# Hybrid decoder block: the denominators of forgetting attention by GpSimd, the first filler's weights loaded sooner, the last norm by halves

## The chip, the cores and the metric

The kernel runs on one core of one Trainium2 chip. A core has five engines with a queue of instructions each: TensorE (PE, matrix products, with a second queue PEld for weight loads), VectorE (DVE), ScalarE (ACT), GpSimd (POOL) and SyncE (SP, used here to issue transfers). Operands live in SBUF, products are summed in eight PSUM banks of 128 partitions by 512 float32, and the large tensors are in HBM. Engines wait for each other by semaphores. The metric is the device time of one execution in microseconds (us); smaller is better.

## What is computed

One decoder layer on 1024 tokens of width 1024, all in float32: two attentions side by side on the same normed input, merged by gates, then a SwiGLU feed-forward part and a final norm.

```python
h = rms_norm(x, norm_mix_g)
proj = h @ w_in                                   # q, k, v of both attentions, forget logits, gates
# dilated attention: 3 groups (window, dilation) x 4 heads of 64, softmax with ALiBi bias,
# the groups mixed by the softmax of their log-sum-exp -> o_a
# forgetting attention: 8 heads of 64, causal
c = cumsum(log_sigmoid(f_logit))                  # per head, along the sequence
logit[t, s] = q[t] . k[s] / sqrt(64) + c[t] - c[s]    for s <= t
o_b = softmax(logit) @ v
merged = sigmoid(..) * (o_a @ w_dil_out) + sigmoid(..) * (o_b @ w_fox_out)
x = x + merged @ w_out
gu = rms_norm(x, norm_ffn_g) @ w_ffn_in           # 2 x 2816 columns
x = x + (silu(gu[:, :2816]) * gu[:, 2816:]) @ w_ffn_down
out = rms_norm(x, norm_final_g)
```

## The kernel before

Float32 precision comes from splitting: an operand is written as a rounded part (`hi`, by ACT, L99) and a remainder (`lo`, by DVE, L102), and a product becomes three products with 128x512 moving operands: hi by hi, hi by lo, lo by hi (L110 to L112, or L315 in the block products `prod`). Large projections are computed from 2x2 blocks with seven block products instead of eight (`projections`, L315). So almost all the time is a row of 128x512 products on PE.

The program runs in stages: value projections and the norm (to about 130 us), the other projections (to about 311 us), forgetting attention (to about 511 us), dilated attention (from 485 us, overlapping, to 621 us), merge and output projection, the feed-forward part, and from 1424 us the rest of the final norm.

**Forgetting attention** has eight units: four head pairs `pr` times two halves `b` of the queries. For a unit, `fox_scores` (L700 on) computes for each head of the pair the scores of 512 queries against 4 or 8 blocks of 128 keys, keys on the partitions: two products each (L713, L714) into a bank, a copy with bias by ACT (L717) into the tile `L`, a causal mask by POOL on diagonal blocks (L720), and a running maximum over key blocks by DVE (L727) into one quarter of the tile `mx`. Then POOL takes the maximum over the 128 partitions (L728, a `partition_all_reduce`, whose result stands in every partition). `fox_values` belongs to the unit before: `fox_exp` subtracts the maximum (DVE, L741 and L744), takes the exponential (ACT, L747), and sums the exponentials over key blocks into the same quarter of `mx` (DVE, L751 and L753). Then come the products with the values (L765) into the bank `po`, and two products of a 128x64 tile of ones with the two heads' sums (L769) into the bank `den`: they add the sums over the 128 partitions and put each head's denominator on its 64 partitions of the bank. `finish` (L371 on) turns `den` into a reciprocal, by Ln and Exp on ACT (L378, L379, tile `rc`) and one Newton step on DVE (L381, L382), and scales `po` with it (L384); POOL issues the store.

Between these products stand **fillers** (`ahead`, L240): projections that attention itself does not need yet (gate columns, and two of the dilated attention's keys, the list `BESIDE`), 48 products each, into banks `pf`. They give PE work while a softmax is under way. The order of each engine's queue is set when the program is built, by a list scheduler that simulates the engines with its own costs, and by explicit constraints (`issue_after`: not before a given instruction; the list `beside` holds the steps of the fillers, to be interleaved). The first filler's weights are loaded by SP (L123), split by ACT and DVE (L99, L102) and used from 290.94 us on, among the last block products and the first scores.

**Dilated attention** follows the same pattern: a maximum over partitions by POOL (L860), sums by DVE (L876), values (L916) and its own products of ones (L922), which the change leaves alone.

**The final norm** works row block by row block of 128 tokens as the last products come out. For each half of 512 columns, DVE adds the bank to the residual (L1359) and ACT squares it with a sum over the row (L1429), which writes the squares into `xf` as well. After the second half, DVE adds the two sums (L1433) and multiplies the whole row of 1024 by the gain into `xf` (L1434); `rstd` takes the square root on ACT (L150) and the rest on DVE (L147, L151 to L160); then ACT and DVE scale a half each (L1439, L1441), and two transfers store them (L1443).

Of the kernel before, what the change touches and what calls it, by code (L numbers as in the profile page):

```python
# [8 lines left out]
F32 = mybir.dt.float32  # L9
F32R = mybir.dt.float32r  # L10
# [37 lines left out]
def layer_kernel(  # L48
# [60 lines left out]
    def mm3(psum, w, m, start, stop):  # L109
        nc.tensor.matmul(psum, w.hi, m.hi, start=start, stop=False)  # L110
        nc.tensor.matmul(psum, w.hi, m.lo, start=False, stop=False)  # L111
        last_mm[0] = nc.tensor.matmul(psum, w.lo, m.hi, start=False, stop=stop)  # L112
# [6 lines left out]
    def load_w(src, kt, n, tag="w", pool=None, rpool=None):  # L119

        hi, lo = [(pool or wpool).tile([P, kt, -(-n // P) * P], F32R, tag=tag + h, name=nm("w" + h), bufs=2) for h in "hl"]
        raw = (rpool or wpool).tile([P, kt, n], F32, tag="wr", name=nm("wr"), bufs=2)
        last_w[0] = nc.sync.dma_start(out=raw[:], in_=src.rearrange("(k p) c -> p k c", p=P))  # L123
        split(hi[:], lo[:], raw[:])
        return Pair(hi, lo)
# [114 lines left out]
    def ahead(pool, c0, dst, dl=1, sc=1.0):  # L240

        pf = [psf.tile([P, HALF], F32, tag="f", name=nm("pf")) for _ in range(2)]
        w = load_w(w_in[:, c0:c0 + P], KT, P)
        steps = []
        for hh in range(2):
            for k in range(KT):
                mm3(pf[hh][:], w[:, k], hT[hh][:, k], k == 0, k == KT - 1)
                steps.append(last_mm[0].ins)
        beside.append(steps)
        n = HALF // dl  # L250
        for hh in range(2):
            st = pool.tile([P, dl, n], F32, tag="fst", name=nm("fst"), bufs=2)
            stored.append(nc.scalar.activation(out=st[:], in_=view(pf[hh][:], dl), func=AF.Copy, scale=sc).ins)
            nc.scalar.dma_start(out=residues(dst, dl, hh), in_=st[:])
# [32 lines left out]
    def left_side(pool, rg, ru, bufs, a22_bufs=2, first=False):  # L287
# [20 lines left out]
        with tc.issue_after(s12_hi[0].ins) if first else ExitStack():  # L308
            return A1, S12, fill(S34, s34[:]), fill(A22, u2)

    def prod(bank, a, b, first=False):
        for k in range(4):
            w, m = a[:, k], b[:, k]
            for n, (p, q) in enumerate(((w.hi, m.hi), (w.hi, m.lo), (w.lo, m.hi))):
                last_mm[0] = nc.tensor.matmul(bank[:], p, q, start=first and k == 0 and n == 0,  # L315
                                              stop=k == 3 and n == 2, skip_group_check=True)

    def projections(pool, T, c, dst, dls, sc, hl=False, first=False):

        T1, T2, T3, T4 = T  # L320

        def put(i, hh, op):

            st = pool.tile([P, dls[i], HALF // dls[i]], F32, tag="qo", name=nm("qo"), bufs=4)
            op(st[:], dls[i])
            if hl:
                flat = st[:].rearrange("p r i -> p (r i)")
                hi = pool.tile([P, HALF], F32R, tag="qh", name=nm("qh"), bufs=2)
                split(hi[:], flat, flat)
                d = dst[i][:, :, hh * HALF:(hh + 1) * HALF]  # L330
                nc.scalar.dma_start(out=d[0], in_=hi[:].bitcast(F32))
                nc.gpsimd.dma_start(out=d[1], in_=flat)
            else:
                nc.gpsimd.dma_start(out=residues(dst[i], dls[i], hh), in_=st[:])

        cc, v2, v3 = [pool.tile([P, HALF], F32, tag=n, name=nm(n), bufs=1) for n in ("cc", "v2", "v3")]
        A1, S12, S34, A22 = left_side(pool, *[raw_w(w_in[:, c0:c0 + P]) for c0 in c], 1, 2, first)
        b1, b2, b3 = pd(), pd(), pd()

        def copy(out, bank, r=1):  # L340
            nc.scalar.activation(out=out, in_=view(bank[:], r), func=AF.Copy, scale=sc)  # L341

        def join(out, bank, other, r=1):
            p, q = view(bank[:], r), view(other[:], r)
            if sc == 1.0:
                nc.vector.tensor_tensor(out=out, in0=p, in1=q, op=ALU.add)
            else:
                nc.vector.scalar_tensor_tensor(out=out, in0=p, scalar=sc, in1=q, op0=ALU.mult, op1=ALU.add)

        flat = view(cc[:], 1), view(v2[:], 1), view(v3[:], 1)  # L350
        prod(b1, A1[:, :4], B11, True)
        with tc.issue_after(s12_hi[0].ins) if first else ExitStack():
            copy(flat[0], b1)
        prod(b2, S12[:, 4:], T2, True)
        join(flat[1], b2, cc)
        prod(b1, A1[:, 4:], B21)
        put(0, 0, lambda o, r: copy(o, b1, r))
        prod(b2, S34[:, :4], T3)
        join(flat[2], b2, cc)
        prod(b3, S12[:, :4], T1, True)  # L360
        put(1, 1, lambda o, r: join(o, b3, v3, r))
        prod(b2, A22, T4)
        put(1, 0, lambda o, r: join(o, b2, cc, r))
        prod(b3, S34[:, 4:], B22)
        put(0, 1, lambda o, r: join(o, b3, v2, r))
# [251 lines left out]
    w0_ctx.__exit__(None, None, None)  # L617

    with pool_of("proj", 1) as upool:
        reserve(upool, ("qh", [HALF], F32R, 2), *[("a22" + n, [4, P], F32R, 2) for n in "hl"],  # L620
                *[(t, [HALF], F32, 1) for t in ("cc", "v2", "v3")], ("qo", [HALF], F32, 4),
                *[("s34" + n, [KT, P], F32R, 1) for n in "hl"], ("pad", [HALF], F32, 1))
        for pr in range(0, 4, 2):
            for a in range(2):
                c0 = FOX0 + a * FOX_W + pr * P
                projections(upool, T, (c0, c0 + P), [fqk_dram[a, pr + i] for i in range(2)], (1, 1),
                            (SCALE, 1.0)[a], True, pr + a == 0)
        for two in TWOS:
            projections(upool, T, [dil_cols(*t) for t in two], [dqk_dram[t] for t in two],
                        [STR[a][g] for u, g, a in two], (SCALE, 1.0)[two[0][2]])  # L630

# [16 lines left out]
    with pool_of("attention", 1) as apool:  # L650
# [104 lines left out]
        def fox_values(pool, scs, pr, b):  # L755

            nj = 4 * b + 4
            for sc in scs:
                fox_exp(sc, b)
            po, den = pd(), pd()  # L760
            fox_valued.append([])
            for j in range(nj - 1, -1, -1):
                for e in (1, 0):
                    L, _, width, off = scs[e]
                    fox_valued[-1].append(nc.tensor.matmul(  # L765
                        po[half[e], HALF - width[j]:], vf[j // 4][:, j % 4, pr, e], L[:, off[j]:off[j + 1]],
                        start=(j == nj - 1), stop=(j == 0), skip_group_check=True).ins)
            for e in (1, 0):
                nc.tensor.matmul(den[half[e], :], ones[:, :64], scs[e][1], start=True, stop=True)  # L769
            o = pool.tile([P, HALF], F32, tag="o", name=nm("o"), bufs=2)  # L770
            finish(pool, po, den, o[:])
            nc.gpsimd.dma_start(out=o_dram[2 + pr, :, b * HALF:(b + 1) * HALF], in_=o[:])
# [524 lines left out]
    with pool_of("down", 1) as fpool, pool_of("early", 1, side="right") as epool:  # L1297
# [121 lines left out]
        with tc.issue_after(last_xr[0].ins):  # L1419
            nc.gpsimd.dma_start(out=gainf[:], in_=norm_final_g.unsqueeze(0).broadcast_to([P, D]))  # L1420
        parts = {}

        def last_rows(t, ch, out, pt):
            add(out, pt)
            if ch == 0:
                parts["xf"] = fpool.tile([P, D], F32, tag="xf", name=nm("xf"), bufs=3)
            xf = parts["xf"]
            sq = parts[ch] = small.tile([P, 1], F32, tag="sq", name=nm("sq"))
            nc.scalar.activation(out=xf[:, ch * HALF:(ch + 1) * HALF], in_=out, func=AF.Square, accum_out=sq[:])  # L1429
            if ch == 0:  # L1430
                return
            ss = small.tile([P, 1], F32, tag="ss", name=nm("ss"))
            nc.vector.tensor_tensor(out=ss[:], in0=parts[0][:], in1=parts[1][:], op=ALU.add)  # L1433
            nc.vector.tensor_tensor(out=xf[:], in0=acc[t][:], in1=gainf[:], op=ALU.mult)  # L1434
            r = rstd(ss, True)
            for c in range(2):
                cs = slice(c * HALF, (c + 1) * HALF)
                if c == 0:
                    nc.scalar.activation(out=xf[:, cs], in_=xf[:, cs], func=AF.Copy, scale=r[:, 0:1])  # L1439
                else:  # L1440
                    nc.vector.tensor_scalar(out=xf[:, cs], in0=xf[:, cs], scalar1=r[:, 0:1],  # L1441
                                            scalar2=None, op0=ALU.mult)
                (nc.scalar, nc.sync)[c].dma_start(out=out_rows(t)[:, cs], in_=xf[:, cs])  # L1443
# [34 lines left out]
```

## Time and profile before

| | us |
|---|---|
| median of 3 runs (lowest, highest) | 1437.19 (1435.22, 1440.91) |
| the profiled execution | 1435.33 |
| its span in the trace | 1432.6 |
| time around the span (difference) | 2.7 |

| stage, us from the span's start | PE busy | DVE busy | ACT busy | POOL busy |
|---|---|---|---|---|
| 280 to 310, last projections | 30.00 of 30 | 12.51 | 4.76 | 12.38 |
| 620 to 1424, merge to last product | 803.77 of 804 | 488.70 | 296.77 | 297.08 |

The table's rows come from one question about busy time in windows; a PE that is busy in all of a window means that products followed each other there without a gap. The windows of the attention stages are shown with the prediction. A 128x512 product is shown as 389 ns long, but they are pipelined: in a row of them one starts every 0.227 us.

### The profile page before, as it was taken

The numbers are of one execution on the slowest core, as the hardware profiler recorded it, in microseconds if no ns is written. First come the engines' busy times: TensorE is split into PE (matmuls) and PEld (weight loads), VectorE is DVE, ScalarE is ACT, GpSimd is POOL, SyncE is SP. The second block draws the span as 40 slices with busy tenths as digits, with TensorE's granted clock in tenths as the row PEclk, the third lists the DMA queues.
The fourth block names the chain that finished last, engine by engine and source line by source line (L and its number), as shares of the span: only waits on it lengthen the run. The fifth ranks groups of instructions, "written<-read, shape, count | busy, mean of one in ns | idle before, by whom it ended". The sixth has DMA issues, their size and how long they took to land.

```text
span 1432.6 us, 18278 instructions
## 1 busy us (share of the span) xinstructions
PE 1421.4 (99%) x6826; PEld 1154.6 (81%) x6826; DVE 946.9 (66%) x1331; ACT 564.0 (39%) x841; POOL 486.6 (34%) x435
## 2 busy tenths in 40 slices
PE   9999999999999999999999999999999999999997
PEld 7888888887776777778888888888888888888886
DVE  6484654459989899967547755565555665765755
ACT  5333433236666523454235522223232233534333
POOL 1021444435434212100454145666666664000000
PEclk9999999999999999999999999999999999999999
DMA  7232444475534462345796223223332332966512
GB/s 243 67 111 75 153 162 125 129 223 133 140 112 118 147 235 67 120 160 176 288 355 253 74 81 103 95 91 101 101 105 97 110 125 96 390 220 226 203 40 80
DMA packets 162407, 212.51 MB, mean 148 GB/s; under 512 B 13712, under 2 KB 110992, under 8 KB 162064
## 3 DMA queue, kind: packets, MB, share of 16 engines
q1 hardware_dynamic: 126304, 119.06, 26.1%
q0 software_dynamic: 15040, 54.54, 10.5%
q10 hardware_dynamic: 20976, 37.76, 8.3%
q8 instruction: 53, 0.87, 0.2%
q14 instruction: 34, 0.28, 0.1%
HBM read 145.79 MB, written 65.54 MB: 148 GB/s over the span
## 4 chain that ended last, share of the span: by engine, by line
PE 95%; DVE 3%; DMA 1%; ACT 0%; issue 0%; POOL 0%; SPq 0%; DVEq 0%; POOLq 0%
PE pd L315 31%; PE pd L1393 11%; PE pf L315 8%; PE pd L110 6%; PE pd L111 6%; PE pd L112 6%; PE pf L110 4%; PE pf L112 4%; PE pf L111 4%; PE pd L203 2%; PE pd L207 2%; PE pd L204 2%; PE pd L765 2%; PE pd L713 1%; PE pd L916 1%; PE pd L714 1%
## 5 line engine op out<-in xcount | busy, mean ns | idle before, releaser
L315 PE MATMUL pd<-tT,wh 128*128 128x512 f32 x768 | 234.8, 389 | 0.0
L102 DVE TENSOR_TENSOR wl<-wr,wh 128x1024 fp32r<-128x1024 f32 (+2 forms) x106 | 125.0, 1181 | 112.2 <-ACT wh L99 112.0
L99 ACT ACTIVATE wh<-wr 128x1024 fp32r<-128x1024 f32 (+2 forms) x106 | 91.1, 861 | 261.3 <-PE pd L315 170.0
L315 PEld LDWEIGHTS pd<-tT,wh 128*128 128x128 f32 x768 | 144.1, 188 | 29.9
L315 PE MATMUL pd<-hT_t,wh 128*128 128x512 f32 x536 | 165.5, 389 | 0.0
L315 PE MATMUL pd<-tT,wl 128*128 128x512 f32 x384 | 147.6, 389 | 0.0
L315 PEld LDWEIGHTS pd<-hT_t,wh 128*128 128x128 f32 x536 | 100.4, 188 | 21.2 <-ACT cc L341 0.2
L110 PE MATMUL pf<-hT_t,wh 128*128 128x512 f32 x288 | 114.3, 397 | 0.0
L111 PE MATMUL pf<-hT_t,wh 128*128 128x512 f32 x288 | 112.5, 391 | 0.0
L112 PE MATMUL pf<-hT_t,wl 128*128 128x512 f32 x288 | 112.3, 390 | 0.0
L99 ACT ACTIVATE wh<-s 128x1024 fp32r<-128x1024 f32 x58 | 61.4, 1060 | 110.0 <-POOL s L302 82.0
L315 PE MATMUL pd<-hT_t,wl 128*128 128x512 f32 x268 | 104.3, 389 | 0.0
L99 ACT ACTIVATE oh<-raw 128x1024 fp32r<-128x1024 f32 x66 | 70.0, 1062 | 81.0 <-PE pd L1393 34.2
L301 POOL TENSOR_TENSOR s<-wr 128x512 f32<-128x512 f32 x29 | 53.3, 1837 | 139.5 <-DMA wr<-in_w_in_dram 67.8
L315 PE MATMUL pf<-hT_t,wh 128*128 128x512 f32 x320 | 98.7, 389 | 0.0
L102 DVE TENSOR_TENSOR wl<-s,wh 128x1024 fp32r<-128x1024 f32 x58 | 71.8, 1239 | 27.7 <-ACT wh L99 27.7
L1393 PE MATMUL pd<-ol,oh 128*128 128x512 f32 x224 | 87.1, 389 | 0.0
L1393 PE MATMUL pd<-oh,ol 128*128 128x512 f32 x224 | 86.3, 389 | 0.0
L1393 PE MATMUL pd<-oh 128*128 128x512 f32 x224 | 84.7, 389 | 0.0
L315 PEld LDWEIGHTS pd<-tT,wl 128*128 128x128 f32 x384 | 72.1, 188 | 15.0
L1085 POOL TENSOR_TENSOR r<-r 128x512 f32<-128x512 f32 x32 | 43.7, 1379 | 116.2 <-DVE wl L102 95.9
L102 DVE TENSOR_TENSOR ol<-raw,oh 128x1024 fp32r<-128x1024 f32 x66 | 76.5, 1221 | 6.6 <-ACT oh L99 6.3
(331 smaller groups left out, 3228.8 us busy)
## 6 DMA issues: line engine op xcount, KB each, us to landing
wr<-in_w_in_dram SPq DMA_DIRECT2D x46, 512.0 KB, 4.6
wr<-in_w_ffn_in_dram SPq DMA_DIRECT2D x44, 512.0 KB, 3.8
raw<-left_dram SPq DMA_DIRECT2D x56, 256.0 KB, 5.3
g_dram<-fst ACTq DMA_DIRECT2D x32, 256.0 KB, 2.2
r<-in_w_ffn_down_dram SPq DMA_DIRECT2D x8, 1024.0 KB, 8.9
right_dram<-r POOLq DMA_DIRECT2D x8, 1024.0 KB, 7.4
left_dram<-f POOLq DMA_DIRECT2D x8, 1024.0 KB, 4.7
raw<-right_dram SPq DMA_DIRECT2D x32, 256.0 KB, 5.4
```

The source lines that it names most:

```text
L99: last_hi[0] = nc.scalar.activation(out=hi, in_=src, func=AF.Copy)
L102: last_lo[0] = nc.vector.tensor_tensor(out=lo, in0=src, in1=hi.bitcast(F32), op=ALU.subtract)
L110: nc.tensor.matmul(psum, w.hi, m.hi, start=start, stop=False)
L111: nc.tensor.matmul(psum, w.hi, m.lo, start=False, stop=False)
L112: last_mm[0] = nc.tensor.matmul(psum, w.lo, m.hi, start=False, stop=stop)
L203: nc.tensor.matmul(pt[hh][:], w.hi[:, k], m.hi, start=(k == 0), stop=False)
L204: nc.tensor.matmul(pt[hh][:], w.hi[:, k], m.lo, start=False, stop=False)
L207: nc.tensor.matmul(pt[hh][:], w.lo[:, k], m.hi, start=False, stop=(k == kt - 1))
L301: nc.gpsimd.tensor_tensor(out=s12[:, :4], in0=u1, in1=u2, op=ALU.add)
L315: last_mm[0] = nc.tensor.matmul(bank[:], p, q, start=first and k == 0 and n == 0, stop=k == 3 and n == 2, skip_group_check=True)
L1085: nc.gpsimd.tensor_tensor(out=out, in0=p, in1=q, op=ALU.subtract)
L1393: nc.tensor.matmul(bank[:], p, q, start=new and n == 0 and i == 0, stop=n == last and i == 2, skip_group_check=True)
```

## The change

Three edits.

1. In `fox_values`, the products of ones are gone. For each head, POOL sums the head's quarter of `mx` over the partitions with an add `partition_all_reduce` in place (new L776). The two heads' results stand in full in two quarters; ACT copies the second head's on partitions 64 to 127 into the first quarter (new L778, a copy of 64x512), and `finish` reads that quarter instead of a PSUM bank. A unit takes one PSUM bank instead of two.
2. The weights of the first filler are loaded ahead, right after the load of the weights of the last but one pair of projections (`TWOS[-2]`), into the space of the `qh` tiles, and are split there; `ahead` takes them from `w_beside`. `qh` becomes one tile with two halves that are used in turn. The products of the first filler are placed not before a given block product (the 49th from the end, `block_steps[-49]`), and `prod` records its products for that.
3. In the last norm, ACT's squares go to a tile of their own (`squares`, from the ring of three `xf` buffers), and DVE multiplies each half by the gain right after its add, instead of the full row after both.

```diff
     def ahead(pool, c0, dst, dl=1, sc=1.0):
-        w = load_w(w_in[:, c0:c0 + P], KT, P)
+        w = w_beside.pop() if w_beside else load_w(w_in[:, c0:c0 + P], KT, P)
...
             for k in range(KT):
-                mm3(pf[hh][:], w[:, k], hT[hh][:, k], k == 0, k == KT - 1)
+                with ExitStack() if beside else tc.issue_after(block_steps[-49]):
+                    mm3(pf[hh][:], w[:, k], hT[hh][:, k], k == 0, k == KT - 1)
...
     def projections(pool, T, c, dst, dls, sc, hl=False, first=False):
-                hi = pool.tile([P, HALF], F32R, tag="qh", name=nm("qh"), bufs=2)
-                split(hi[:], flat, flat)
+                hi = qh[0][:, len(puts) % 2]
+                puts.append(i)
+                split(hi, flat, flat)
...
     with pool_of("proj", 1) as upool:
+        qh[0] = upool.tile([P, 2, HALF], F32R, tag="qh", name=nm("qh"), bufs=1)
...
+            if two is TWOS[-2]:
+                raw0 = upool.tile([P, KT, P], F32, tag="qh", name=nm("wr"), bufs=1)
+                with tc.issue_after(last_w[0].ins):
+                    nc.sync.dma_start(out=raw0[:], in_=w_in[:, dil_cols(*BESIDE[0]):dil_cols(*BESIDE[0]) + P].rearrange(
+                        "(k p) c -> p k c", p=P))
+        w_beside = [pair_of(raw0[:])]
...
         def fox_values(pool, scs, pr, b):
-            po, den = pd(), pd()
+            po = pd()
+            for sc in scs:
+                nc.gpsimd.partition_all_reduce(sc[1], sc[1], P, bass_isa.ReduceOp.add)
+            den = scs[0][1]
+            nc.scalar.activation(out=den[half[1], :], in_=scs[1][1][half[1], :], func=AF.Copy)
...
-            for e in (1, 0):
-                nc.tensor.matmul(den[half[e], :], ones[:, :64], scs[e][1], start=True, stop=True)
             o = pool.tile([P, HALF], F32, tag="o", name=nm("o"), bufs=2)
             finish(pool, po, den, o[:])
...
+        squares = fpool.tile([P, HALF], F32, tag="xf", name=nm("xf"), bufs=3)
         def last_rows(t, ch, out, pt):
             add(out, pt)
...
-            nc.scalar.activation(out=xf[:, ch * HALF:(ch + 1) * HALF], in_=out, func=AF.Square, accum_out=sq[:])
+            nc.scalar.activation(out=squares[:], in_=out, func=AF.Square, accum_out=sq[:])
+            hs = slice(ch * HALF, (ch + 1) * HALF)
+            nc.vector.tensor_tensor(out=xf[:, hs], in0=out, in1=gainf[:, hs], op=ALU.mult)
...
-            nc.vector.tensor_tensor(out=xf[:], in0=acc[t][:], in1=gainf[:], op=ALU.mult)
             r = rstd(ss, True)
```

How the queues stand now, at three places. The first is PE at the end of the first unit's values (`pd` are banks, `v` the values, `L` the exponentials, `qx`, `ql`, `kx` the next scores' operands). Before:

```order
L765 MATMUL pd_413_2700<-L_390_2536,v_383_2454 64x512
L765 MATMUL pd_413_2700<-L_385_2502,v_383_2454 64x512
L769 MATMUL pd_414_2701<-mx_2451,ones_88 64x512 x2
L713 MATMUL pd_419_2732<-qx_2448,kx_2449 128x512
L714 MATMUL pd_419_2732<-ql_2450,kx_2449 128x512
```

After:

```order
L783 MATMUL pd_399_2689<-L_376_2525,v_369_2443 64x512
L783 MATMUL pd_399_2689<-L_371_2491,v_369_2443 64x512
L727 MATMUL pd_404_2721<-qx_2437,kx_2438 128x512
L728 MATMUL pd_404_2721<-ql_2439,kx_2438 128x512
L727 MATMUL pd_405_2729<-qx_2437,kx_2438 128x384
```

The two products of ones are gone, and the next scores follow the values directly.

The second place is POOL in the middle of forgetting attention: masks (`AFFINE_SELECT`) of the scores of the units to come, maxima (ISA at L728 before, L742 now), denominators (ISA at L776) and stores. Before:

```order
L720 AFFINE_SELECT L_456_3027<-L_456_3027 128x128 x4
L720 AFFINE_SELECT L_461_3061<-L_461_3061 128x128 x4
L728 ISA mx_2451<-mx_2451 128x512
L772 DMA o_dram_81<-o_453_3008 128x512
L728 ISA mx_2451<-mx_2451 128x512
L772 DMA o_dram_81<-o_468_3153 128x512
L720 AFFINE_SELECT L_471_3162<-L_471_3162 128x128 x4
```

After:

```order
L734 AFFINE_SELECT L_439_3016<-L_439_3016 128x128 x4
L734 AFFINE_SELECT L_444_3050<-L_444_3050 128x128 x4
L742 ISA mx_2440<-mx_2440 128x512 x2
L776 ISA mx_2440<-mx_2440 128x512 x4
L734 AFFINE_SELECT L_453_3151<-L_453_3151 128x128 x4
L788 DMA o_dram_81<-o_450_3142 128x512
```

The denominators of two units (four all-reduces) now stand one behind the other between the maxima and the next masks, and the store of the earlier of these units stands behind the masks.

The third place is ACT near the same kind of point, one pair of heads earlier: score copies with bias (`negc`), exponentials in place (`L<-L`), and the reciprocal (`rc`). Before:

```order
L747 ACTIVATE L_395_2570<-L_395_2570 128x1024 x2
L378 ACTIVATE rc_417_2714<-pd_414_2701 128x512
L747 ACTIVATE L_395_2570<-L_395_2570 128x512
L717 ACTIVATE L_418_2731<-pd_419_2732,negc_98 128x512
L747 ACTIVATE L_395_2570<-L_395_2570 128x384
L717 ACTIVATE L_418_2731<-pd_420_2740,negc_98 128x384
```

After:

```order
L731 ACTIVATE L_408_2754<-pd_409_2755,negc_98 128x512
L761 ACTIVATE L_381_2559<-L_381_2559 128x256
L778 ACTIVATE mx_2440<-mx_2440 64x512
L761 ACTIVATE L_381_2559<-L_381_2559 128x128
L385 ACTIVATE rc_402_2703<-mx_2440 128x512
L731 ACTIVATE L_408_2754<-pd_410_2763,negc_98 128x384
L386 ACTIVATE rc_402_2703<-rc_402_2703 128x512
```

The copy of the second head's denominators stands between exponentials and score copies and waits there for POOL; the reciprocal, which stood between the tile's exponentials of 1024 and of 512 columns, stands behind its last one, and its second half behind one more score copy.

More of the change, by code (lines that the diff above doesn't have):

```diff
@@ L309, in left_side @@
             return A1, S12, fill(S34, s34[:]), fill(A22, u2)
+    block_steps = []
     def prod(bank, a, b, first=False):
@@ L316, in prod @@
                                               stop=k == 3 and n == 2, skip_group_check=True)
+                block_steps.append(last_mm[0].ins)
+    qh, puts = [None], []
     def projections(pool, T, c, dst, dls, sc, hl=False, first=False):
@@ L327, in put @@
                 flat = st[:].rearrange("p r i -> p (r i)")
-                hi = pool.tile([P, HALF], F32R, tag="qh", name=nm("qh"), bufs=2)
-                split(hi[:], flat, flat)
+                hi = qh[0][:, len(puts) % 2]
+                puts.append(i)
+                split(hi, flat, flat)
                 d = dst[i][:, :, hh * HALF:(hh + 1) * HALF]
-                nc.scalar.dma_start(out=d[0], in_=hi[:].bitcast(F32))
+                nc.scalar.dma_start(out=d[0], in_=hi.bitcast(F32))
                 nc.gpsimd.dma_start(out=d[1], in_=flat)
@@ L619, in layer_kernel @@
     with pool_of("proj", 1) as upool:
-        reserve(upool, ("qh", [HALF], F32R, 2), *[("a22" + n, [4, P], F32R, 2) for n in "hl"],
+        qh[0] = upool.tile([P, 2, HALF], F32R, tag="qh", name=nm("qh"), bufs=1)
+        reserve(upool, *[("a22" + n, [4, P], F32R, 2) for n in "hl"],
                 *[(t, [HALF], F32, 1) for t in ("cc", "v2", "v3")], ("qo", [HALF], F32, 4),
```

## The prediction

> **What bounds the kernel now.** I read the page first: busy time by engine, the slices, the chain.
>
> ```profile
> span 1432.6 us, 18278 instructions
> PE 1421.4 (99%) x6826; PEld 1154.6 (81%) x6826; DVE 946.9 (66%) x1331; ACT 564.0 (39%) x841; POOL 486.6 (34%) x435
> DVE  6484654459989899967547755565555665765755
> PE 95%; DVE 3%; DMA 1%; ACT 0%; issue 0%; POOL 0%; SPq 0%; DVEq 0%; POOLq 0%
> ```
>
> PE is busy for all but 11 us at the span's ends, and the chain is PE's. Taking work off PE therefore pays one for one, as long as no other engine becomes late. The third line shows who could: DVE has eight slices in a row at 8 and 9 tenths, the tenth to the seventeenth of 40, or 322 to 609 us: the attention, which is where the change works. So I asked for busy time in windows there, one for each unit of forgetting attention and one for the dilated attention behind it. The columns are PE, PEld, DVE, ACT and POOL, with counts, then granted clock, DMA share and GB/s.
>
> ```profile
> 334.00:357.00 23.00, 23.00 (x113) 17.69 (x112) 22.23 (x37) 17.39 (x34) 11.83 (x15) 1.00 0.50 124
> 357.00:380.00 23.00, 23.00 (x112) 15.86 (x111) 20.58 (x44) 12.47 (x24) 7.68 (x9) 1.00 0.39 119
> 380.00:403.00 23.00, 23.00 (x115) 17.83 (x114) 22.36 (x37) 17.41 (x32) 13.27 (x15) 1.00 0.57 145
> 403.00:426.00 23.00, 23.00 (x112) 15.86 (x111) 18.28 (x37) 11.99 (x23) 6.51 (x9) 1.00 0.31 96
> 426.00:449.00 23.00, 23.00 (x115) 17.83 (x114) 21.39 (x34) 17.14 (x32) 12.26 (x15) 1.00 0.62 146
> 449.00:472.00 23.00, 23.00 (x112) 15.86 (x111) 18.98 (x39) 11.76 (x23) 6.84 (x9) 1.00 0.40 127
> 472.00:495.00 23.00, 23.00 (x145) 16.83 (x144) 21.81 (x39) 12.91 (x22) 7.70 (x7) 1.00 0.49 171
> 495.00:518.00 23.00, 23.00 (x134) 15.34 (x133) 22.45 (x33) 6.56 (x12) 6.20 (x5) 1.00 0.52 180
> 518.00:620.00 102.00, 101.94 (x711) 78.50 (x710) 99.22 (x159) 39.29 (x57) 15.70 (x14) 1.00 0.38 130
> ```
>
> Over the first eight, 184 us, DVE is busy 168.08 and idle 15.92; in the last it is idle 2.78. So DVE is 18.7 us short of being the bound over 286 us. PE has no gap, but only just.
>
> **What leaves PE: 7.2 us.** The group of the products of ones, one unit in the timeline, and the last unit:
>
> ```profile
> L769 PE MATMUL pd<-mx,ones x32: 592/592/643, 340.3 to 510.5; 128*64 128x512 f32 x32
> 340.30 1.03 PE L769 MATMUL pd<-mx,ones 128*64 128x512 f32 x4
> 341.26 0.50 PE L713 MATMUL pd<-qx,kx 128*128 128x512 f32 x1
> 509.99 1.08 PE L769 MATMUL pd<-mx,ones 128*64 128x512 f32 x4
> 511.00 1.18 PE L393 MATMUL pd<-kx 64*128 64x128 f32 x16
> ```
>
> The 32 records are four in each of eight units. From the first of them to the next product 0.96 us pass, in the last unit 1.01. The switch from 64-column to 128-column products stays, and I estimate 0.1 us of each 0.96 for it. So 8 × 0.86 = 6.9 us at least and 7 × 0.96 + 1.01 = 7.7 at most; I take 7.2.
>
> **What comes to POOL, ACT and DVE.** The sum by POOL isn't in this trace, only the same instruction for the maximum, and ACT's copy only at twice the partitions:
>
> ```profile
> L728 POOL PARTITION_ALL_REDUCE mx<-mx x16: 1782/2144/2269, 323.1 to 484.8; - x16
> 280.31 0.60 ACT L341 ACTIVATE qo<-pd 128x512 f32<-128x512 f32 x1 [4.59 <-PE pd L315]
> ```
>
> Sixteen sums at 2.14 us are 34 us of POOL, 4.3 a unit. POOL's fullest window above holds 13.27 of 23, so 17.6 of 23 with them: no bound by itself. The eight copies add 4.8 us to an ACT whose fullest window holds 17.41. Both are covered as amounts; their places are not, see the rivals. If a sum took 4 us instead, POOL would still fit, at 21.3 of 23.
>
> On DVE nothing is added, but its instructions stretch while POOL reduces. One place, POOL's row first, then DVE's under it, then the same shape without POOL:
>
> ```profile
> 336.45 2.20 POOL L728 PARTITION_ALL_REDUCE mx<-mx  x1
> 336.93 1.25 DVE L753 TENSOR_TENSOR mx<-mx,L 128x256 f32<-128x256 f32 x1
> 344.20 0.42 DVE L727 TENSOR_TENSOR mx<-mx,L 128x256 f32<-128x256 f32 x1
> ```
>
> One operation with two SBUF inputs took 1.25 instead of 0.42: 0.83 us. Adding up such excess under all sixteen maxima, instruction by instruction against the usual length of its shape, I get 10.6 us, 0.66 each. Sixteen sums should cost DVE another 10.6. From below, nothing, if the sums fall on DVE's idle time; from above, 16 × 0.83 = 13.3.
>
> [...]
>
> DVE's idle time has to take up the 10.6. What the idle time is made of:
>
> ```profile
> L727 DVE TENSOR_TENSOR mx<-mx,L 128x512 f32<-128x512 f32 (+3 forms) x56 | 28.8, 519 | 6.9 <-POOL L L720 3.4 <-ACT L L717 2.3
> L381 DVE TENSOR_TENSOR den<-pd,rc 128x512 f32<-128x512 f32 x7 | 4.8, 686 | 4.1 <-ACT rc L379 4.1
> ```
>
> The 4.1 us before L381 are waits for the reciprocal. They go where the new order puts other work ahead of it, and come back where it doesn't: the reciprocal now needs sums on DVE, two reductions and a copy on POOL and ACT, then Ln and Exp. In the new DVE queue I find it well covered at most units, and close behind the sums at two or three, 1 to 3 us each. The 6.9 before L727 are waits for masks and score copies, and stay in part, since masks now queue behind up to four sums (8.6 us). So of 18.7 us idle I let DVE keep the 2.8 of the dilated attention, half of the 6.9 (3.5) and 2.4 for reciprocals: R = 8.7, with 2.8 and 18.7 (all) as ends.
>
> How late may DVE be? The last place where PE meets it:
>
> ```profile
> L922 PE MATMUL pd<-mx,ones x16: 592/618/643, 537.6 to 621.1; 128*64 128x512 f32 x16
> L876 DVE TENSOR_TENSOR mx<-mx,over x16: 673/688/721, 536.6 to 615.1; 128x512 f32<-128x512 f32 x16
> ```
>
> PE's last product of ones there begins at 621.1 (the first of its four at 620.7), DVE's last sum ends at 615.8: a margin of 4.8 us. PE now comes 7.2 earlier, so DVE must finish 2.4 us earlier than before to cost nothing. If DVE keeps idle time R, its end moves by 10.6 − (18.7 − R), and PE waits R − 5.7 us. With 8.7 that is **3.0 us** given back; R below 5.7 gives back nothing.
>
> **The first filler: 0.** Its load, split and first use before:
>
> ```profile
> 281.53 9.65 SPq L123 DMA_DIRECT2D wr<-in_w_in_dram  x3
> 288.46 1.06 ACT L99 ACTIVATE wh<-wr 128x1024 fp32r<-128x1024 f32 x1 [7.55 <-DMA wr<-in_w_in_dram]
> 289.55 1.23 DVE L102 TENSOR_TENSOR wl<-wr,wh 128x1024 fp32r<-128x1024 f32 x1 [3.79 <-ACT wh L99]
> 290.94 0.39 PE L110 MATMUL pf<-hT_t,wh 128*128 128x512 f32 x1
> 291.85 0.39 PE L713 MATMUL pd<-qx,kx 128*128 128x512 f32 x1
> 294.12 0.33 PE L713 MATMUL pd<-qx,kx 128*128 128x384 f32 x1
> 280.00:310.00 30.00, 30.00 (x134) 24.83 (x134) 12.51 (x15) 4.76 (x6) 12.38 (x19) 1.00 0.92 249
> ```
>
> The split ends at 290.78, 0.16 us before the first filler, but PE is busy 30.00 of 30, so a sooner load has no wait to remove. What hides it is PE's row of products. The price is in what moves up: in the new order two scores (512 and 384 queries) and the last twelve block products stand ahead of the filler. If the first score follows at 290.94 it comes 0.9 us sooner than before, and the second, at 291.17, 3.0 sooner than 294.12; operands that landed just in time before would make PE wait that long, 3.0 at most. The load also moves past two others on SP's queue, those of the last projections, with DMA at a share of 0.92 in this window. No row shows such an operand late, so I take 0, with −1 (a DVE that is through with the split sooner, 1.23) and +3 as ends.
>
> **The last norm: −0.8.** The tail:
>
> ```profile
> 1424.31 0.69 DVE L1359 TENSOR_TENSOR acc<-acc,pd 128x512 f32<-128x512 f32 x1 [1.87 <-PE pd L112]
> 1425.03 0.63 ACT L1429 ACTIVATE xf<-acc 128x512 f32<-128x512 f32 x1 [2.06 <-DVE acc L1359]
> 1425.78 0.16 DVE L1433 TENSOR_TENSOR ss<-sq,sq 128x1 f32<-128x1 f32 x1 [0.79 <-ACT xf L1429]
> 1425.89 1.23 DVE L1434 TENSOR_TENSOR xf<-acc,gain 128x1024 f32<-128x1024 f32 x1
> 1425.98 0.29 ACT L150 ACTIVATE t<-ss,epst 128x1 f32<-128x1 f32 x1 [0.23 <-DVE ss L1433]
> 1427.10 0.15 DVE L151 RECIPROCAL y<-t 128x1 f32<-128x1 f32 x1
> ```
>
> The full-row multiply stands between the sum and the reciprocal, which was ready to go at 1425.98 + 0.29 = 1426.27 and went at 1427.10. A half (about 0.62, half of 1.23) now runs beside the square, in the 0.79 us that DVE waits there. So 1427.10 − 1426.3 = 0.8; between 0, if the half delays the sum, and 1.1.
>
> **Sum.** 7.2 + 0.8 − 3.0 − 0 = 5.0 us faster. The profiled execution took 1435.33, 2.7 around its span, and is 1.86 under the median; I place the result beside the median, 1437.19 − 5.0 = 1432.2, rounded to **1432.0**.
>
> **Rivals.**
> (a) DVE keeps less than 5.7 us idle: the whole 8.0, 1429.2. For it: the new queue has fewer instructions that each need the one just before. Against it: the dilated attention's 2.8 can't be used, and masks wait longer.
> (b) DVE becomes the bound, the case on the other side. One mechanism: in the unit where the queue of sums on POOL lies between the last sum on DVE and the reciprocal that DVE waits for, DVE idles. It decides from R = 13.7, where the loss eats all 8.0. With R = 18.7 PE waits 13.0 and the kernel takes 1437.2 − 8.0 + 13.0 = 1442.2. For it: four sums stand in one row on POOL, 8.6 us. Against: at most units tens of DVE instructions stand between.
> (c) POOL shuts DVE out for the whole of each sum: 34 us in place of 10.6 make PE wait R + 17.7 = 26.4, so 1437.2 − 8.0 + 26.4 = 1455.6. Against it: the row at 336.93. [...]
> (d) ACT's copy stands ahead of score copies and waits for POOL, so banks stay full and PE stops at scores: up to 4.3 us for two sums, so 1436.3, or 1440.6 if at two units. Against it: a unit holds one bank less now.
> (e) The change not doing what it says: the new PE queue has no products of ones in forgetting attention, so at most the first filler's edit is empty, which costs nothing.
>
> **Chances.** Forecast (gain 2 to 7) 0.57, (a) 0.25, (b) 0.10, (c) 0.02, (d) 0.06. The range leaves out (c), the worse half of (b), and a little at the fast end: 1427 (7.7 from PE, 1.1 and 1.0 from the other edits, all kept, give 1427.4) to 1441. A measurement here can tell about 0.5%, 7.2 us, from no change. Only (a) passes that on the fast side, so 0.25 faster, 0.68 within, and 0.07 slower, from (b) and (c).
>
> **What would show it.** Right: no L769, next scores directly behind the values; DVE's idle time from 334 to 620 at 8 to 9 us; PE waits of about 3 us in all, from DVE or ACT behind it, in the dilated attention or at its end; the reciprocal of the last norm 0.5 us or less after the square root. Wrong: PE waits at scores for ACT's copy, sums longer than 2.3 us, PE waits between 290 and 308 us, or a DVE excess under sums far from 0.66 us each.

## The result, and the profile after

The changed kernel takes 1458.05 us (median of 4 runs, 1456.60 to 1458.94); the kernel before takes 1436.2 in the same comparison. The ratio is 1.0148, with a 95% interval from 1.013 to 1.0166: 22 us slower, where I had forecast 5 us faster and a range that ended at 1441. In the later comparisons the kernel before has medians of 1434.6 to 1435.1, against which the loss would be 23 us.

From the page of the changed kernel: busy time, DVE's slices and the chain of the end.

```profile
span 1456.2 us, 18240 instructions
PE 1429.9 (98%) x6794; PEld 1161.9 (80%) x6794; DVE 971.8 (67%) x1339; ACT 569.2 (39%) x849; POOL 551.4 (38%) x451
DVE  6484654459989799975726854555665655765665
PE 84%; DVE 9%; issue 2%; POOL 2%; ACT 1%; DMA 1%; ACTq 0%; SPq 0%; DVEq 0%; POOLq 0%
```

PE has 32 instructions fewer and still gains 8.5 us of busy time: part of the rest ran slower. DVE has 25 us more. The chain has gone from 95% PE to 84%, and DVE, POOL and ACT stand in it. Where the time went is seen from one line of PE that both kernels share, 32 products early in the merge behind both attentions (first the kernel before, then the changed one; times are durations in ns, then first and last start in us):

```profile
L203 PE MATMUL pd<-od,wh x32: 389/389/389, 643.6 to 686.2; 128*128 128x512 f32 x32
```

```profile
L203 PE MATMUL pd<-od,wh x32: 388/390/390, 668.0 to 710.6; 128*128 128x512 f32 x32
```

It starts 24.4 us later, as the merge's very first product does (621.7 before, 646.1 after), and the span is 23.6 longer: all of the loss lies ahead of the merge, and 0.8 come back behind it. Busy time in windows of the changed kernel, columns as in the prediction:

```profile
280.00:310.00 30.00, 30.00 (x135) 24.86 (x134) 14.20 (x15) 5.18 (x7) 12.34 (x18) 1.00 0.89 238
334.00:357.00 23.00, 21.44 (x104) 16.43 (x103) 22.55 (x33) 16.06 (x30) 18.04 (x17) 1.00 0.46 113
357.00:380.00 23.00, 19.53 (x90) 12.51 (x89) 22.65 (x34) 7.75 (x17) 14.66 (x6) 0.99 0.30 89
426.00:449.00 23.00, 19.69 (x90) 15.11 (x91) 20.21 (x28) 16.16 (x32) 17.16 (x14) 0.93 0.68 161
472.00:495.00 23.00, 20.02 (x90) 15.52 (x90) 17.74 (x22) 15.51 (x29) 18.02 (x14) 0.93 0.33 111
334.00:518.00 184.00, 172.53 (x829) 125.38 (x827) 168.11 (x266) 107.49 (x201) 118.14 (x87) 0.97 0.42 117
518.00:646.00 128.00, 123.28 (x800) 92.25 (x799) 122.01 (x192) 45.94 (x67) 31.24 (x21) 0.96 0.40 134
```

PE, which had no gap before, now stands still for 11.5 us of the first 184 and 4.7 of the next 128, 16.2 in all. And the granted clock, 1.00 in every window before, falls to 0.93 in windows with a long pause. Behind it are five stretches at half clock, 20.5 us in all, one of them here:

```profile
481.90:485.30 3.40, 3.40 (x11) 2.57 (x10) 1.07 (x1) 2.45 (x7) 3.40 (x2) 0.50 0.40 110
```

Half of 20.5 is 10.2 us, so pauses and clock make 26.4. The merge's 24.4 plus the PE work that was saved (my sum's 7.2) is 31.6. Some 5 us are not assigned; this view makes each pause look shorter than it is, since a product's record (389 ns) is longer than its place in a row (227 ns).

What PE waits for, and the two kinds of reduction on POOL:

```profile
PE pd L727 <- ACT L L731: 9.5, 4, 3.4
PE pd L400 <- DVE over L848: 3.4, 1, 3.4
L776 POOL PARTITION_ALL_REDUCE mx<-mx x16: 3182/3400/4182, 332.1 to 538.5; - x16
L742 POOL PARTITION_ALL_REDUCE mx<-mx x16: 1736/1909/5886, 323.0 to 502.2; - x16
```

A sum over partitions takes 3.40 us (3.46 on average), a maximum over the same 128x512 takes 1.91 (medians). I had put the maximum's 2.14 in its place. And PE waits at scores (L727) for ACT's score copies (L731), 9.5 us in four pauses, and once in the dilated attention for DVE, but not at its end. One such pause, engine by engine, from the timeline (start, length, engine, line, count, and in brackets idle time and its releaser):

```profile
473.22 6.53 POOL L776 PARTITION_ALL_REDUCE mx<-mx  x2
473.35 5.89 DVE L755 TENSOR_TENSOR L<-L,mx 128x512 f32<-128x512 f32 x4 [0.36 <-POOL mx L742]
479.13 0.61 ACT L761 ACTIVATE L<-L 128x256 f32<-128x256 f32 x2 [1.96 <-DVE L L755]
479.65 0.67 ACT L731 ACTIVATE L<-pd,negc 128x512 f32<-128x512 f32 x1
477.01 0.39 PE L110 MATMUL pf<-hT_t,wh 128*128 128x512 f32 x1
480.38 0.45 PE L727 MATMUL pd<-qx,kx 128*128 128x384 f32 x1 [2.98 <-ACT L L731]
482.26 0.64 PE L727 MATMUL pd<-qx,kx 128*128 128x512 f32 x1
482.70 0.63 PE L728 MATMUL pd<-ql,kx 128*128 128x512 f32 x1
485.53 0.39 PE L111 MATMUL pf<-hT_t,wh 128*128 128x512 f32 x1
485.76 0.39 PE L112 MATMUL pf<-hT_t,wl 128*128 128x512 f32 x1
```

Two sums on POOL; under them DVE's four subtractions take 5.89 us, though their shapes (512, 384, 256 and 128 columns, with no POOL beside them 0.69, 0.55, 0.42 and 0.28) make 1.94. ACT's exponentials wait for the subtractions, the score copies stand behind the exponentials in ACT's queue, no bank comes free, and PE stops after 477.01 and goes on at 480.38. From 482.26 its products come every 0.43 us; at 485.53 they are back at 0.23.

### The profile page after: what moved, and what is told of

It reads as the page before. It is cut to its first block, busy times and chain, and to the rows that moved or that the text cites. A ratio compares the mean times of both kernels' runs of the same rounds, so it can differ in the third digit from the quotient of the medians.

```text
span 1456.2 us, 18240 instructions
## 1 busy us (share of the span) xinstructions
PE 1429.9 (98%) x6794; PEld 1161.9 (80%) x6794; DVE 971.8 (67%) x1339; ACT 569.2 (39%) x849; POOL 551.4 (38%) x451
## 4 chain that ended last, share of the span: by engine, by line
PE 84%; DVE 9%; issue 2%; POOL 2%; ACT 1%; DMA 1%; ACTq 0%; SPq 0%; DVEq 0%; POOLq 0%
PE pd L318 30%; PE pd L1409 10%; PE pf L318 7%; PE pd L110 6%; PE pd L111 6%; PE pd L112 6%; PE pf L110 2%; DVE L L755 2%; PE pf L111 2%; PE pf L112 2%; PE pd L203 2%; PE pd L204 2%; PE pd L207 2%; DVE mx L767 1%; DVE L L758 1%
## 5 line engine op out<-in xcount | busy, mean ns | idle before, releaser
L110 PE MATMUL pf<-hT_t,wh 128*128 128x512 f32 x288 | 116.5, 404 | 0.0
L111 PE MATMUL pf<-hT_t,wh 128*128 128x512 f32 x288 | 114.8, 399 | 0.0
L318 PE MATMUL pf<-hT_t,wh 128*128 128x512 f32 x320 | 98.7, 390 | 0.0
```

## Experiments

Theory A: the sum itself is to blame, since it runs longer and holds DVE longer than I had taken. Theory B: the new waits and queue places are. "DVE excess" is the time by which DVE operations were longer than operations of the same shape with no POOL beside them, each counted once, under the operation of POOL that covered most of it; which length is taken as the usual one moves these sums by up to 1.5 us.

**e1 and e5: the maximum in place of the sum.** One word changes, the queue orders stay the same in every row. The denominators become maxima.

```diff
-                nc.gpsimd.partition_all_reduce(sc[1], sc[1], P, bass_isa.ReduceOp.add)
+                nc.gpsimd.partition_all_reduce(sc[1], sc[1], P, bass_isa.ReduceOp.max)
```

> The sum over partitions is replaced by the maximum, so the denominators are maxima of the sums; queue orders and waits are those of the changed kernel. Theory A (the sum itself: it runs 3.46 us where I had 2.14, and holds one DVE operation back for about 2.04 us where I had 0.66): these reductions run 1.8 to 2.3 us, the DVE excess under them falls from 29.4 us to 10 to 14, PE's pauses in the attention from 18 us to under 6, and the time comes to 1432 to 1441 us. Theory B (the new waits, by the place of the reductions and of ACT's copy in the queues): most pauses stay, 1447 to 1456 us.

> The kernel of e1 once more, for its trace. Timed at 1443 to 1446 us, it is neither what theory A nor what theory B gave. Theory A: 16 reductions of 1.8 to 2.3 us, 10 to 14 us of DVE excess under them, and PE's pauses follow the time: 6 to 12 us in the attention, at scores that wait for a bank. Theory B: the excess is the same, and pauses at scores are as long as with the sum, 14 us or more.

e1 took 1445.1 us against 1434.9 before (the median of three executions; a fourth, the traced one, took 7899.2 for a reason that is not known and is left out), ratio 1.0068 (1.0052 to 1.0085). e5, the same kernel run once for a trace, took 1449.9, some 5 us more than e1, so its waits may be a little long. Its reductions:

```profile
L776 POOL PARTITION_ALL_REDUCE mx<-mx x16: 1736/1949/2356, 332.3 to 530.5; - x16
```

The DVE excess under them is 10.7 us, 0.67 each: the term of my sum. With the sum it is 27.0. So the operation alone is worth some 12 us of the loss, and theory A has that part right. But in e5 PE is still idle for 12.4 us between 334 us and the merge (16.2 with the sum), and e1's time lies between what the two theories gave: with my own prices the kernel would still have been 10 us slower than before. Something else in my account was wrong as well.

The traces show a part of it: the hold seems to work the other way round too. In the changed kernel a maximum on POOL stands beside a row of DVE's additions:

```profile
412.33 5.89 POOL L742 PARTITION_ALL_REDUCE mx<-mx  x1 [5.75 <-DVE mx L741]
413.42 3.16 DVE L767 TENSOR_TENSOR mx<-mx,L 128x512 f32<-128x512 f32 x6
418.25 1.53 DVE L755 TENSOR_TENSOR L<-L,mx 128x512 f32<-128x512 f32 x1 [1.68 <-POOL mx L742]
```

The maximum takes 5.89 us instead of 1.91. It ends 1.6 us after DVE's row does, nearly a maximum's whole length, and DVE waits for it. Two more take 4.96 (at 468.4) and 5.49 us (the dilated attention's, at 525.7), and all three stand in the chain of work that ended last. In the kernel before no maximum in the attention takes more than 2.54; e5 has two of 5.89 and 5.49. The new queue orders place such rows of DVE behind a maximum, so this is a price of the order. No run changes it by itself, and I had no term for it.

**e2: no reduction at all.** The two lines of the reduction are taken out, and the logarithm gets a bias of one, so the denominators are unsummed.

```diff
...
-            for sc in scs:
-                nc.gpsimd.partition_all_reduce(sc[1], sc[1], P, bass_isa.ReduceOp.add)
...
```

> The 16 sums over partitions are left out (the reciprocal is taken of the unsummed sums, with one added under the logarithm so that it stays finite); no products of ones either, ACT's copy stays, and the queues are ordered anew. Theory A and theory B: the whole gain of PE and tail, 7 to 9 us, so 1427 to 1430 us, and no pause of PE over 0.6 us. If the loss came from a third cause (fewer banks, the first filler, new order of fillers), pauses stay and the time is over 1436 us.

1433.0 us, ratio 0.9981 (0.9972 to 0.9991): 2 us gained, not 8, against all theories. PE waits here for a load (in all, times, longest):

```profile
PE pd L727 <- DMA qx<-fqk_dram: 2.7, 3, 2.1
```

In the new order PE comes to the scores of a head pair before its `qx` has landed. Between 334 us and the merge PE is idle for 4.0 us, 2.1 of them at one such place. Three maxima on POOL take 5.63, 6.31 and 3.82 us here, without any sum. How the rest of the missing 6 us divides I can't say. So even free sums would have brought no more than 2 us in the order that this program was given.

**e3, e9 and e10: the edits apart.** e3 is the changed kernel with the products of ones put back (edits 2 and 3), e9 the kernel before with edit 1, e10 the kernel before with edit 3; their diffs are parts of the one above.

> The products of ones are back, the first filler's early load and the last norm by halves stay. All theories of edit 1: 1434.5 to 1436.5 us; the tail from the last add to the end is 0.8 us shorter than before, and the early load changes nothing on PE between 280 and 310 us. If the early load were what hurts: over 1440 us.

> The denominators' edit alone. If the three edits add up, 1458.05 plus what edits 2 and 3 gain in e3 (0.9 us): 1457 to 1461 us. If the earlier load of the first filler's weights had a part in the loss, under 1453 us.

> The last norm by halves alone: 0.6 to 0.9 us under the kernel before; if all of the gain of e3 is its own, the same as e3, 0.9992 of the kernel before; if the gain of e3 came from the early load, 1.000.

e3: 1433.9 us, ratio 0.9992 (0.9983 to 1.0001), 0.6 us under the range that I gave. e9: 1457.05, ratio 1.0154 (1.0138 to 1.0171), as expected if the edits add up. e10: 1434.9, ratio 0.9997 (0.9984 to 1.001), which decides between none of its cases. Edit 1 carries the whole loss, and edits 2 and 3 gain at most what can't be told from noise, so of the kernels that compute the whole layer none clearly beats the one before. PE in e3 has no pause over 0.6 us between 280 and 650 us.

**e4: sums that nobody needs.** e3, with the sums on POOL behind the products of ones.

```diff
...
                 nc.tensor.matmul(den[half[e], :], ones[:, :64], scs[e][1], start=True, stop=True)
+            for sc in scs:
+                nc.gpsimd.partition_all_reduce(sc[1], sc[1], P, bass_isa.ReduceOp.add)
```

> As e3, and beside it POOL sums the same quarters over the partitions after the products of ones have read them; nobody reads the result before the quarter is used again two units later. Theory A: DVE operations are stretched by about 2 us under each sum, DVE becomes late although nothing waits for the sums, 1442 to 1455 us. Theory B: nobody waits for a sum, 1435 to 1439 us.

1457.3 us, ratio 1.0155 (1.0138 to 1.0171), above even theory A's range. DVE excess under the sums 30.1 us. PE does all the work that the change had removed, waits for no sum, and the kernel ends where the changed one ends: with DVE held back like this, PE's 7 us are worth nothing. That the result of a sum is waited for isn't needed for the loss. DVE and POOL ahead of a pause of PE at 429.5 us:

```profile
423.42 6.61 POOL L785 PARTITION_ALL_REDUCE mx<-mx  x2 [2.14 <-PE pd L783]
423.59 2.74 DVE L767 TENSOR_TENSOR mx<-mx,L 128x256 f32<-128x256 f32 x2
426.25 3.73 DVE L755 TENSOR_TENSOR L<-L,mx 128x512 f32<-128x512 f32 x4
```

Two additions that need 0.4 each, and four subtractions that need 1.94 together: each group is longer by about 1.9, one sum's hold.

**e6: the hold by itself.** Behind the end of the kernel before, blocks of one POOL operation beside a chain of DVE operations of 128x128, each 0.29 us and one every 0.32.

```diff
...
+            nc.gpsimd.partition_all_reduce(Z[:, :n], A[:, :n], P, getattr(bass_isa.ReduceOp, o))
+            for i in range(32 if n > 512 else 18):
+                if kind == 0:
+                    nc.vector.tensor_tensor(out=B[:, :P], in0=B[:, :P], in1=A[:, :P], op=ALU.add)
+                elif kind == 1:
+                    nc.vector.tensor_scalar(out=B[:, :P], in0=A[:, :P], scalar1=1.0, scalar2=None, op0=ALU.mult)
+                else:
+                    nc.vector.tensor_tensor(out=B[:, :P], in0=Q[:, :P], in1=A[:, :P], op=ALU.add)
```

> The kernel before, and behind its end 16 blocks: one POOL operation beside a chain of small DVE operations of 128x128. Theory A: with two SBUF inputs one DVE operation is held 0.6 to 1.0 us under a maximum of 128x512 and 1.9 to 2.2 us under a sum of 128x512; with fewer columns the sum and the hold shrink, with 1024 they grow; a DVE operation with one input, or with one of two in PSUM, is not held. If the hold is the same for sum and maximum, or as long as the whole reduction, theory A has the wrong mechanism. For memset, copy and mask of 128x512 by POOL there is no expectation beyond their lengths.

The timeline, POOL's row and then DVE's first operations under it, for a maximum of 512 columns, sums of 512, 256 and 1024, a sum of 512 beside one-input operations (L1473), and one beside operations with one input in PSUM (L1475):

```profile
1440.80 1.94 POOL L1468 PARTITION_ALL_REDUCE xf<-xf  x1 [177.24 <-DVE xf L1471]
1440.79 1.34 DVE L1471 TENSOR_TENSOR xf<-xf,xf 128x128 f32<-128x128 f32 x2
...
1461.04 3.33 POOL L1468 PARTITION_ALL_REDUCE xf<-xf  x1 [5.98 <-DVE xf L1458]
1460.99 2.54 DVE L1471 TENSOR_TENSOR xf<-xf,xf 128x128 f32<-128x128 f32 x2
...
1477.53 1.89 POOL L1468 PARTITION_ALL_REDUCE xf<-xf  x1 [6.27 <-DVE xf L1458]
1477.47 1.39 DVE L1471 TENSOR_TENSOR xf<-xf,xf 128x128 f32<-128x128 f32 x2
...
1500.35 6.21 POOL L1468 PARTITION_ALL_REDUCE xf<-xf  x1 [6.53 <-DVE xf L1458]
1500.29 4.83 DVE L1471 TENSOR_TENSOR xf<-xf,xf 128x128 f32<-128x128 f32 x2
...
1516.27 3.28 POOL L1468 PARTITION_ALL_REDUCE xf<-xf  x1 [9.71 <-DVE xf L1458]
1516.21 2.41 DVE L1473 TENSOR_SCALAR xf<-xf 128x128 f32<-128x128 f32 x2
...
1524.64 3.23 POOL L1468 PARTITION_ALL_REDUCE xf<-xf  x1 [5.09 <-DVE xf L1458]
1524.91 0.29 DVE L1475 TENSOR_TENSOR xf<-pd,xf 128x128 f32<-128x128 f32 x1
```

Two free operations take 0.62 together (one spacing and one length). So a maximum holds one operation for 0.72 us, a sum for 1.92, and the sum's hold grows with its columns: 0.77 at 256, 1.92 at 512, 4.21 at 1024. With an operand in PSUM there is none: eleven of them took 3.54 us, one every 0.32. A mask and a copy of 512 columns by POOL each lengthened one DVE operation from 0.29 to 0.58 us, a memset none (four in 1.27 us). I had not expected that one-input operations are held too (2.41 us for two). The hold looks like a full stop of a fixed length: it adds about 1.9 us to an operation of 0.29 us here and to the longer ones in e4. It covers only part of the reduction (1.92 of 3.33 us).

**e7: POOL as busy, without the hold.** Six memsets of the quarter to 1.0 in place of each sum, 16 × 6 of them. ACT's copy and the waits for POOL stay.

```diff
-                nc.gpsimd.partition_all_reduce(sc[1], sc[1], P, bass_isa.ReduceOp.add)
+                for _ in range(6):
+                    nc.gpsimd.memset(sc[1], 1.0)
```

> The changed kernel with each sum over partitions replaced by six memsets of the quarter to 1.0, so the denominators are ones; ACT's copy and the waits for POOL stay, the queues are ordered anew. By the blocks of e6 six memsets keep POOL busy for 3.1 us, as long as a sum, but hold no DVE operation. Theory A (the hold): DVE excess under them below 3 us in all, 1429 to 1438 us. Theory B (POOL's occupied queue and the waits for its results): as long as with the sums, 1446 to 1458 us.

**e8: a short sum.** Sums of 128 of the 512 columns, so most denominators stay unsummed, with the bias of e2.

```diff
-                nc.gpsimd.partition_all_reduce(sc[1], sc[1], P, bass_isa.ReduceOp.add)
+                nc.gpsimd.partition_all_reduce(sc[1][:, :P], sc[1][:, :P], P, bass_isa.ReduceOp.add)
...
```

> The changed kernel with sums over partitions of 128 of the 512 columns only; the other denominators stay unsummed, with one added under the logarithm so that it is finite. The queue orders are nearly those of the changed kernel, ACT's copy and the waits stay. By e6 such a sum takes 1.17 us and holds DVE 0.2. Theory A: about 3 us of DVE excess, 1431 to 1440 us. Theory B: the orders decide, 1443 to 1456 us.

e7: 1440.7 us, ratio 1.004 (1.0026 to 1.0054). e8: 1439.3, ratio 1.0031 (1.002 to 1.0043). The memsets in e7 (lengths in ns):

```profile
L777 POOL MEMSET mx<- x96: 517/527/601, 332.1 to 526.8; 128x512 f32 x96
```

POOL is as busy as with the sums (6 × 0.53 = 3.2 us each), and the result is waited for in the same way, but beside the kernel before it loses 6.1 us instead of 21.9. DVE excess is 7.1 us in e7, where theory A gave under 3, and 3.9 in e8. Nearly 5 of e7's 7.1 are a one-input copy (3.42 us) and the addition behind it, under a row of ten memsets; the memset blocks of e6 had only two-input operations and don't cover this case. e8 lies in theory A's range, e7 2.7 us above it, and neither reaches B's. The queues of e2, e4, e7 and e8 were ordered anew when they were built, so their differences are not pure prices. In e8, against what I had expected of it, 316 of DVE's 1339 instructions stand at another place in the queue than in the changed kernel, as many as in e2 (323). Only e1 and e5 have the changed kernel's orders.

The runs in one table. DVE's and PE's times are from 334 us to the first product of the merge. The longest maximum is that of forgetting attention. e1's time stands beside e5's trace; e5 itself took 15.1 us more than its kernel before.

| kernel | DVE excess under the added operation | DVE busy | DVE idle | PE idle | longest maximum on POOL | us above the kernel before |
|---|---|---|---|---|---|---|
| before | none | 268.9 | 18.8 | 0.1 | 2.27 | 0 |
| e3, no edit 1 | none | 268.9 | 18.6 | 0.1 | 2.27 | −1.0 |
| e2, no sum | none | 265.2 | 21.2 | 4.0 | 6.31 | −1.9 |
| e8, sum of 128 columns | 3.9 | 271.5 | 22.8 | 8.4 | 5.56 | 4.7 |
| e7, memsets | 7.1 | 270.2 | 24.3 | 6.6 | 5.63 | 6.1 |
| e1/e5, maximum | 10.7 | 273.4 | 30.8 | 12.4 | 5.89 | 10.2 |
| changed | 27.0 | 290.2 | 21.9 | 16.2 | 5.89 | 21.9 |
| e4, unused sum | 30.1 | 297.2 | 14.3 | 15.6 | 2.88 | 22.4 |

By e1 and e5 the longer hold and length of the sum are some 12 of the 22 us. The other 10 come from holds like a maximum's, the new order and its waits together, and no run parts these.

## Why the prediction was wrong, point by point

**What bounds the kernel: right, and too short.** PE was the bound by a thin margin, with DVE 18.7 us behind it over 286. The change moved the bound to DVE with ACT and POOL in its loop.

**What leaves PE, 7.2 us: gone as forecast, and worth nothing.** The products are gone from PE (32 instructions less; no run shows their 7.2 us by itself). The switch to 128-column products stays: the first score behind the values is 0.50 us long in both kernels (at 341.26 and 340.14), 0.11 more than in a row, near the 0.1 of my estimate. e4, which still has the products of ones, ends within 1 us of the changed kernel.

**A sum as long as a maximum, 2.14 us: wrong.** It takes 3.46. That was the first of two mis-sized terms; I took the nearest row for an operation with another reduction in it, and took the upper end of its hold from a maximum as well. POOL had room for it, as I had said for 4 us; the price came through DVE.

**DVE's excess, 10.6 us with 13.3 as upper end: the term that failed most.** It measured 27.0. The 0.66 each was right for a maximum, where e5 gives 0.67. For a sum it is 1.7 on average in the kernel and 1.92 in e6. My reading of the row at 336.93 was wrong too. The operation there began 0.48 us after the reduction and ended 0.47 before it, and I took it for one that was slowed over its length; by e6, where a maximum adds 0.72 us to an operation of 0.29, it was held for a while and then ran. Rival (c) had the mechanism, at 34 us instead of 27, and its 1455.6 us is the nearest to what came; I gave it 2 in 100 because of that reading. That it came so near is in part luck: it took the whole of a reduction that it put at 2.14 us, where about half of 3.46 was held.

**Idle time that DVE can use up, R = 8.7 of 18.7: wrong.** DVE's idle time was 18.8 us before, 21.9 after, and 14 to 31 in every kernel that had something added. As I read it now, it is not a stock. It stands between steps of a loop (scores on PE, copies on ACT, maxima on DVE and POOL, subtraction on DVE, exponentials on ACT), and a longer step anywhere in the loop moves the waits along with it; the wait of 1.68 us for the long maximum at 418.25 is one of them. By the sum as I wrote it, with PE's wait as excess + R − 16.3 (which is R − 5.7 at an excess of 10.6), 27.0 and 21.9 give 32.6 us, and 31.6 were found (24.4 at the merge and the 7.2). That this closes is bookkeeping, since an engine's busy and idle time fill the window; it says that the two inputs were mis-sized and not why. In e5 the excess is the one that I had forecast, and an idle time of 30.8 stands where I had put 8.7.

**Where DVE meets PE: wrong.** I looked for the last meeting, in the dilated attention, with a margin of 4.8 us. PE stopped for the first time near 342 us, behind the first unit's values, for a load:

```profile
342.80 0.47 PE L727 MATMUL pd<-qx,kx 128*128 128x512 f32 x1 [1.11 <-DMA qx<-fqk_dram]
```

Without the products of ones the scores begin 1.1 us sooner (340.14 against 341.26), and the `qx` of this one had not landed. From 374 us on it stopped at scores that waited for a bank: the path of rival (d), but with the subtractions under the sum at its root. ACT's copy itself was waited for once, 4.3 us, by DVE.

**The clock: left out.** PE's pauses cost themselves and some 10.2 us more at a lower clock (half of the 20.5 us at 0.50). My rows held no pause of PE in the attention, so none of them showed it.

**The signs.** Of those that I had named as showing me wrong, three came: PE waiting at scores for ACT's copies, sums longer than 2.3 us, and a DVE excess far from 0.66 each. The fourth, pauses between 290 and 308 us, did not come in the changed kernel.

**The first filler, 0: right for the executions that I had traced, but my reason was too short.** PE is busy 30.00 of 30 between 280 and 310 us in both, and e9, without the early load, loses as much as the changed kernel (1.0154 and 1.0148). But the trace of e10, which hasn't the early load either, is of a longer execution (1439.67 us, against e10's median of 1434.9):

```profile
292.49 1.06 ACT L99 ACTIVATE wh<-wr 128x1024 fp32r<-128x1024 f32 x1 [11.58 <-DMA wr<-in_w_in_dram]
293.59 0.80 PE L110 MATMUL pf<-hT_t,wh 128*128 128x512 f32 x1 [2.49 <-ACT wh L99]
```

The split begins 4.0 us later than in the prediction's row (288.46), because the load landed late; PE pauses for 2.49 us and the granted clock is 0.51 in the next 3.4. With the early load nothing is left there to wait for. Of the 63 executions of e10 and of the kernel before, 17 took more than 1437 us; of the 20 of e3 and e2, which load early, none did. That the other long ones had the same wait is likely but not traced. So the early load seems to gain in these long executions, where a median hardly shows it.

**The last norm, −0.8: right.** The tail of the changed kernel:

```profile
1448.75 0.69 DVE L1375 TENSOR_TENSOR acc<-acc,pd 128x512 f32<-128x512 f32 x1 [1.98 <-PE pd L112]
1449.47 0.69 DVE L1448 TENSOR_TENSOR xf<-acc,gain 128x512 f32<-128x512 f32 x1
1450.29 0.16 DVE L1452 TENSOR_TENSOR ss<-sq,sq 128x1 f32<-128x1 f32 x1
1450.81 0.16 DVE L151 RECIPROCAL y<-t 128x1 f32<-128x1 f32 x1 [0.17 <-ACT t L150]
```

From the last add to the reciprocal 2.06 us pass, 2.79 before: 0.7 gained, and the half took 0.69 instead of my 0.62. From that add to the span's end it is 7.45 us after and 8.29 before. In e10 alone such a gain can't be told from noise.

## What to carry to other kernels

Before work is moved from a full engine to an idle one, ask which third engine's operations grow longer beside it: here each 128x512 sum on POOL held DVE for up to 1.9 us (e6), and DVE was, next to PE, the engine with the least room. Price an operation from a row of the same operation; the same instruction with another reduction inside took 1.7 times as long and held DVE 2.7 times as long (e6). And don't count the idle time of a nearly full engine as room when it stands between the steps of a loop that other engines close: here at most 4.5 of 18.8 us were used (e4). Last, the edit gave every queue a new order, and the order had prices of its own (late loads, long maxima) that no term of the sum held.

## What the runs showed of the hardware that I had not expected

- A sum over partitions of 128x512 takes 3.3 us and a maximum 1.9, and they hold DVE for 1.92 and 0.72 us (e6). The hold is shorter than the reduction. Beside a sum it also caught DVE operations with a single SBUF input (2.41 us for two), and not those with an operand in PSUM (eleven in 3.54 us).
- Beside a row of DVE operations on SBUF a maximum on POOL took 5.89 us instead of 1.91, and ended 1.6 us after the row. In e6's rows of short DVE operations POOL was not kept waiting like this (1.94 us); what decides is not shown.
- After a pause PE's products came at about half their rate: every 0.43 us instead of 0.23 from 482.26 to 484.84, after a pause of 3 us that had ended at 480.38. Two shorter pauses close together were followed by the same (PE's rows of the changed kernel's timeline; a length of 0.63 instead of 0.39 marks the slow products):

```profile
376.46 0.45 PE L727 MATMUL pd<-qx,kx 128*128 128x384 f32 x1 [2.11 <-ACT L L731]
378.74 0.39 PE L727 MATMUL pd<-qx,kx 128*128 128x256 f32 x1 [0.96 <-ACT L L731]
379.76 0.63 PE L110 MATMUL pf<-hT_t,wh 128*128 128x512 f32 x1
```

The granted clock was 0.50 from 379.60 to 382.90 and from 481.90 to 485.30. The slow stretch lasted 3.4 us at both places and began only after PE had gone on, 0.8 us after 378.74 and 1.5 us after 480.38. PE stood still for 2.98 us ahead of one such stretch, for 2.49 us ahead of another (e10), and for 2.11 and 0.96 us with products between them ahead of a third; what decides is not shown.
